# The 64-expert stage: second products in plain float32, subtractions on VectorE, outputs evicted on ScalarE, the gate at the end, empty slots not gathered

## The chip, the cores and the metric

One core of one Trainium2 chip runs the whole program. The metric is the device time of the core in microseconds (us). The time before is 3594.27 us, the median of 3 runs (3585.16 to 3597.85). Engines are named as in the profile: PE is TensorE, DVE is VectorE, ACT is ScalarE, POOL is GpSimd, SP is SyncE, which issues the weight loads.

## What is computed

The reference is two transformer blocks one after the other on 512 tokens of width 1024. Everything in the change lies in the last stage, the feed-forward part of the second block: 64 experts in 8 groups, 8 experts for each token, and one shared expert. Cut to that:

```python
def moe_ffn(h, router_w, router_bias, w_gu, w_dn, w_sh_gu, w_sh_dn):
    t = h.reshape(B * S, D)                                # 512 x 1024
    scores = jax.nn.sigmoid((t @ router_w).astype(jnp.float32))
    ...                                                    # top 4 of 8 groups, then top 8 experts
    top_w = top_w / jnp.sum(top_w, axis=-1, keepdims=True) * ROUTED_SCALE
    routed = routed_experts(t, top_i, top_w, w_gu, w_dn)   # 64 experts, hidden 256
    shared = swiglu(t, w_sh_gu, w_sh_dn).astype(jnp.float32)
    return (routed + shared).reshape(B, S, D).astype(h.dtype)

x = x + g2 * moe_ffn(...)          # g2 is the gate, one number for each of the 1024 columns
return rmsnorm_2(x, final_g)
```

512 tokens times 8 experts are 4096 pairs, so an expert has 64 tokens on average.

## The kernel before, in words

The stage is the class `Moe64`; its `run` is called last, after a stage that mixes tokens. The residual `xT` and the normed input `hT` lie transposed in SBUF (features on partitions).

Prologue: `start` turns the residual to token rows and writes it to a DRAM tensor `sum` of 512 + 128 rows (the last 128 are spare rows; their first content does not matter). `tokens` writes the normed input as rows to the DRAM tensor `rows`. `route` does the routing, a long run of small VectorE instructions. `shared_up` does the first product of the shared expert.

Then a loop over 65 blocks of 128 slots: one for each of the 64 experts, and one (`EXTRA`) that takes a second block of an expert with more than 128 tokens. The weights of an expert are three units of 1 MB (two of the first product, one of the second), each a [128, 2048] float32 tile. They come on SP's queue into a ring of slots (L240); a slot is loaded again when its last reader is done. In block e the program does, in this order:

- `up(e)`: 8 calls of `product`, one for each 128 rows of the contraction. `product` splits the weight piece (128x512 float32) in two float32r halves that together keep its precision: a copy on ScalarE rounds it (L532), and a subtraction makes the rest (L533), every third time on GpSimd, else on VectorE. Then come three matmuls (L2401, L2402, L2403). The two halves have four buffers each (`PIECES`). Silu on ScalarE (L2411) and a multiplication on VectorE (L2412) follow.
- `spread` of the output of block e - 2 (L2438): GpSimd issues a DMA that adds 128 rows of 4 KB to the rows of `sum` at the places `dst`. Each of these waits on GpSimd's queue until the one before it has landed, since both write `sum`. Empty slots (64 of 128 on average) add zeros to the spare rows.
- `down(e - 1)`: for each half of the columns two `product` calls, so 4 in all, and one VectorE instruction that multiplies by the slot's weight and by the gate row (L2433) into `y`, which has 3 buffers.
- `turn(e + 1)`: 8 transposes of the gathered rows and their split into two halves from PSUM (ScalarE and VectorE, 128x512, twice).
- `fetch(e + 4)`: a one-hot compare on VectorE (L2362), 4 small matmuls, six small VectorE instructions that make the slots' row numbers, and an indirect DMA on GpSimd's queue (L2378) that gathers 128 rows of 4 KB from `rows`; empty slots gather row 0. `AHEAD` is 4.
- `turn_hid(e)`: two transposes and their split (128x256).
- in blocks 4, 8, 12 and 16 also `shared_down`: 4 float32 matmuls (L2353) and 2 VectorE evictions with the gate into `sh`.

At the end, SP loads `sum` back (L2518), and for each of four row tiles VectorE adds `sh` (L2520), ScalarE squares and sums (L2521), VectorE scales (L2523) and SP stores the output.

The order within an engine is set ahead of time by priorities from this program order, so an instruction can move forward past others of its engine, but each engine then runs its list in order. An earlier stage, `HierMoe` (32 experts), gathers rows with the bounds check that the change brings here: an index beyond the last row moves nothing (L1357).

## Time and profile before

| | us |
|---|---|
| median of 3 runs | 3594.27 |
| the profiled execution | 3588.4 |
| its span in the trace | 3586.7 |
| stretch of the 65 blocks, first scatter-add to last (L2438) | 2763.0 to 3560.6 |
| PE, DVE, ACT, POOL busy over the span | 3167.3, 2079.6, 1510.7, 940.1 |

The page shows the span in 40 slices of 89.7 us; the stage of the change fills slices 31 to 40. Matmuls overlap each other in the records, so their spacing tells more than their length. A record of a DMA queue counts the time of its packets as a share of 16 DMA engines.

### The profile page before, as it was taken

How to read it: one execution, taken by the hardware profiler on the slowest of the kernel's cores; microseconds unless marked ns; L12 is line 12 of the kernel's file. 1: busy time of each engine (PE TensorE's matmuls, PEld its weight loads, DVE VectorE, ACT ScalarE, POOL GpSimd, SP SyncE). 2: the span in 40 equal slices, each digit the busy share in tenths (PEclk: the TensorE clock that was granted, in tenths of full speed). 3: DMA queues.
4: the chain of work that ended last, by engine and by line, in shares of the span. 5: the costliest groups of instructions: out<-in, count | busy, mean ns of one | idle time of the engine just before them, and what ended most of it. 6: DMA issues, size and time to landing. Idle time of an engine off the chain costs nothing. (4 is left out here: it accounts for less than half of the span.)

```text
span 3586.7 us, 46891 instructions
## 1 busy us (share of the span) xinstructions
PE 3167.3 (88%) x17204; PEld 1966.6 (55%) x17204; DVE 2079.6 (58%) x4291; ACT 1510.7 (42%) x2849; POOL 940.1 (26%) x932
## 2 busy tenths in 40 slices
PE   7888989979998998999899995899998888888885
PEld 4666767643333336763333332676565666666663
DVE  3677673543334335343333334564647999999996
ACT  5555554521111113331111111554545667777775
POOL 3544332100000000000000001221003666666664
PEclk9988999979999998989999997899999999999998
DMA  4111233468999993558999993114236999999996
GB/s 168 54 54 39 68 119 119 183 268 350 413 386 394 371 378 144 188 192 356 397 401 374 367 374 149 72 59 153 95 125 211 331 330 331 337 339 340 334 337 173
DMA packets 140714, 885.09 MB, mean 247 GB/s; under 512 B 19136, under 2 KB 19904, under 8 KB 46784
## 3 DMA queue, kind: packets, MB, share of 16 engines
q1 hardware_dynamic: 103824, 748.73, 53.5%
q0 software_dynamic: 34208, 124.28, 12.0%
q10 hardware_dynamic: 2448, 9.04, 0.7%
q8 instruction: 137, 2.24, 0.3%
q14 instruction: 97, 0.79, 0.1%
HBM read 836.10 MB, written 55.57 MB: 249 GB/s over the span
## 5 line engine op out<-in xcount | busy, mean ns | idle before, releaser
L532 ACT ACTIVATE phase<-arena 128x512 fp32r<-128x512 f32 (+1 forms) x989 | 608.9, 622 | 450.0 <-PE ps L545 196.6
L533 DVE TENSOR_TENSOR phase<-arena,phase 128x512 fp32r<-128x512 f32 (+1 forms) x663 | 612.0, 939 | 128.4 <-ACT phase L532 122.4
L533 POOL TENSOR_TENSOR phase<-arena,phase 128x512 fp32r<-128x512 f32 (+1 forms) x454 | 514.2, 1134 | 589.2 <-ACT phase L532 492.2
L545 PE MATMUL ps<-phase 128*128 128x512 f32 (+3 forms) x1000 | 394.6, 395 | 1.0 <-POOL phase L533 1.0
L1412 PE MATMUL ps<-arena 128*64 128x512 f32 x1008 | 346.3, 614 | 45.2 <-DVE arena L1402 45.2
L2403 PE MATMUL ps<-phase 128*128 128x512 f32 x780 | 312.7, 401 | 64.0 <-DVE phase L533 64.0
L2402 PE MATMUL ps<-phase 128*128 128x512 f32 x780 | 321.3, 412 | 45.1 <-DVE phase L533 33.9
L2401 PE MATMUL ps<-phase 128*128 128x512 f32 x780 | 312.7, 401 | 6.9 <-ACT phase L532 1.5
L1390 PE MATMUL ps<-arena,phase 128*64 128x512 f32 x968 | 303.6, 624 | 2.2 <-ACT phase L1369 0.7
L1390 PE MATMUL ps<-arena 128*64 128x512 f32 x1008 | 303.2, 617 | 1.9 <-DVE arena L1435 0.2
L544 PE MATMUL ps<-phase 128*128 128x512 f32 (+1 forms) x736 | 283.1, 385 | 24.0 <-DVE arena L1710 14.7
L1357 POOL DMA_INDIRECT phase<-hrows,phase x35 | 34.9, 997 | 951.0 <-DVE arena L1393 664.3
L546 PE MATMUL ps<-phase 128*128 128x512 f32 (+1 forms) x736 | 279.5, 380 | 1.1 <-POOL phase L533 1.1
L1392 ACT ACTIVATE arena<-ps 64x512 f32<-64x512 f32 x34 | 20.0, 589 | 477.1 <-PE ps L1390 477.1
L2402 PEld LDWEIGHTS ps<-phase 128*128 128x128 f32 x780 | 146.5, 188 | 128.8 <-DVE phase L533 64.6
L545 PEld LDWEIGHTS ps<-phase 128*128 128x128 f32 (+2 forms) x1000 | 192.4, 193 | 37.6 <-issue 3.3
L2403 PEld LDWEIGHTS ps<-phase 128*128 128x128 f32 x780 | 146.8, 188 | 113.6 <-DVE phase L533 89.5
L1435 DVE SCALAR_TENSOR_TENSOR arena<-ps,arena 128x512 f32<-128x512 f32 x280 | 190.7, 744 | 16.7 <-PE ps L1434 15.5
L1412 PEld LDWEIGHTS ps<-arena 128*64 128x64 f32 x1008 | 93.4, 138 | 179.6 <-issue 130.4
L1354 DVE COPY phase<-ps 128x2 f32<-128x2 f32 (+1 forms) x35 | 5.6, 159 | 304.7 <-PE ps L1352 303.6
L2401 PEld LDWEIGHTS ps<-phase 128*128 128x128 f32 x780 | 146.8, 188 | 48.5 <-ACT phase L532 18.5
L1390 PEld LDWEIGHTS ps<-arena 128*64 128x64 f32 x1008 | 87.6, 142 | 154.5 <-issue 148.6
(625 smaller groups left out, 5818.1 us busy)
## 6 DMA issues: line engine op xcount, KB each, us to landing
arena<-in_moe SPq DMA_DIRECT2D x550, 1024.0 KB, 8.8
arena<-in_ada SPq DMA_DIRECT2D x72, 1024.0 KB, 6.5
phase<-in_moe SPq DMA_DIRECT2D x26, 1024.0 KB, 11.3
arena<-in_wina SPq DMA_DIRECT2D x16, 1024.0 KB, 4.8
arena<-in_win SPq DMA_DIRECT2D x13, 1024.0 KB, 5.1
arena<-in_winb SPq DMA_DIRECT2D x12, 1024.0 KB, 5.8
arena<-in_wouta SPq DMA_DIRECT2D x4, 1024.0 KB
arena<-in_woutb SPq DMA_DIRECT2D x4, 1024.0 KB, 5.6
```

Source lines behind the costliest of these rows:

```text
L532: self.nc.scalar.activation(h, x, AF.Copy)
L533: (eng or self.nc.vector).tensor_tensor(l, x, h, op=OP.subtract)
L544: mm(ps, w[0], x[0], start=start, stop=False)
L545: mm(ps, w[0], x[1], start=False, stop=False)
L546: mm(ps, w[1], x[0], start=False, stop=stop)
L1357: nc.gpsimd.indirect_dma_start(out=x, out_offset=None, in_=self.rows[:], in_offset=bass.IndirectOffsetOnAxis(ap=idx[:n, :1], axis=0), boun ...
L1390: nc.tensor.matmul(ph[64 * j:64 * j + 64, :], x[:, k, :], u, start=k == 0, stop=k == 7)
L1412: nc.tensor.matmul(py[64 * j:64 * j + 64, :], hT[:, k, :], u, start=k == 0, stop=k == 3)
L1435: nc.vector.scalar_tensor_tensor(xT[:, f, :], ps, gate[:, f:f + 1], xT[:, f, :], op0=OP.mult, op1=OP.add)
L2401: nc.tensor.matmul(ps, x[0], h, start=start, stop=False)
L2402: nc.tensor.matmul(ps, x[0], l, start=False, stop=False)
L2403: nc.tensor.matmul(ps, x[1], h, start=False, stop=stop)
```

## The change

- `down` multiplies the hidden values as plain float32 with the weights as they were loaded: one float32 matmul (128x128 by 128x512) in place of a split and three float32r matmuls, 4 in place of 12 per block. `turn_hid` then only copies the transposed hidden values (ScalarE) and has no subtraction.
- `product` makes the rest (the subtraction) always on VectorE.
- The result of `down` is evicted by ScalarE with the slot's weight as its scale (2 instructions of 128x512); the gate is not applied there.
- `sum` starts with zeros (5 DMAs of a zeroed tile); the residual's rows go to another DRAM tensor `xrow`, from where one DMA on ScalarE's queue loads them into `sh`. `shared_down` adds the gated shared output to it (one more VectorE instruction per half). At the end VectorE multiplies the loaded sum by the gate, 4 instructions of 128x1024.
- `fetch` gives empty slots a row number beyond the last, with the bounds check, so that they are not gathered; the four tiles that receive the rows are zeroed once by GpSimd. The scatter-add still sends 128 rows.

```diff
--- before.py
+++ after.py
@@ -2168,7 +2168,6 @@
 EXTRA = 1
 SHARED = 4, 8, 12, 16
 PIECES = 4
-SHARE = 1, 3
 FAR = 1048576.0
 
 
@@ -2178,7 +2177,6 @@
 
     def __init__(self, K):
         self.K, self.nc, self.tc = K, K.nc, K.tc
-        self.turns = 0
 
     def route(self, hT):
         K, nc, a = self.K, self.nc, self.K.a
@@ -2317,6 +2315,9 @@
 
         K, nc = self.K, self.nc
         self.sum = K.dp.tile([T + P, D], F32, name="sum", bufs=1)
+        self.xrow = K.dp.tile([P, 4, D], F32, name="xrow", bufs=1)
+        for i in range(5):
+            nc.gpsimd.dma_start(self.sum[P * i:P * i + P], self.xr[0])
         for i in range(4):
             t = K.a.rot("tok", [P, D], 2)
             for half in range(2):
@@ -2324,8 +2325,7 @@
                 for k in range(4):
                     nc.tensor.transpose(p[:, P * k:P * k + P], xT[:, 4 * half + k, P * i:P * i + P], K.ident)
                 nc.scalar.activation(t[:, 512 * half:512 * half + 512], p, AF.Copy)
-            nc.gpsimd.dma_start(self.sum[P * i:P * i + P], t)
-        nc.gpsimd.dma_start(self.sum[T:], t)
+            nc.gpsimd.dma_start(self.xrow[:, i, :], t)
 
     def shared_up(self, hT):
 
@@ -2352,7 +2352,9 @@
             for k in range(2):
                 nc.tensor.matmul(p, self.hid[:, k, P * i:P * i + P], self.dn[:, 1024 * k + 512 * half:1024 * k + 512 * half + 512],
                                  start=k == 0, stop=k == 1)
-            nc.vector.tensor_tensor(self.sh[:, i, c], p, self.gate[:, c], op=OP.mult)
+            t = K.t2k()
+            nc.vector.tensor_tensor(t, p, self.gate[:, c], op=OP.mult)
+            nc.vector.tensor_tensor(self.sh[:, i, c], self.sh[:, i, c], t, op=OP.add)
 
     def fetch(self, pos, info):
 
@@ -2369,14 +2371,16 @@
         idx, dst = a.rot("idx", [P, 2], AHEAD + 2).bitcast(I32)[:, 0:1], a.rot("dst", [P, 2], AHEAD + 2).bitcast(I32)[:, 0:1]
         w = a.rot("w", [P, 1], AHEAD + 2)
         V.tensor_tensor(s[:, 6:7], s[:, 0:1], s[:, 1:2], op=OP.add)
-        V.tensor_copy(idx, s[:, 6:7])
         V.tensor_reduce(out=w, in_=s[:, 2:5], op=OP.add, axis=AX.X)
 
         V.tensor_scalar(s[:, 7:8], s[:, 5:6], -1.0, 1.0, op0=OP.mult, op1=OP.add)
+        V.scalar_tensor_tensor(idx, s[:, 7:8], 4096.0, s[:, 6:7], op0=OP.mult, op1=OP.add)
         V.scalar_tensor_tensor(dst, s[:, 7:8], self.spare, s[:, 6:7], op0=OP.mult, op1=OP.add)
-        x = a.rot("xr", [P, D], AHEAD)
+        self.row += 1
+        x = self.xr[self.row % AHEAD]
         nc.gpsimd.indirect_dma_start(out=x, out_offset=None, in_=self.rows[:],
-                                     in_offset=bass.IndirectOffsetOnAxis(ap=idx[:, :1], axis=0))
+                                     in_offset=bass.IndirectOffsetOnAxis(ap=idx[:, :1], axis=0),
+                                     bounds_check=T - 1, oob_is_err=False)
         return x, w, dst
 
     def turn(self, x):
@@ -2396,8 +2400,7 @@
 
         K, nc = self.K, self.nc
         h, l = (K.r.rot(n, [P, 512], PIECES) for n in ("wh", "wl"))
-        self.turns += 1
-        K.parts(h, l, w, nc.gpsimd if self.turns % SHARE[1] < SHARE[0] else nc.vector)
+        K.parts(h, l, w)
         nc.tensor.matmul(ps, x[0], h, start=start, stop=False)
         nc.tensor.matmul(ps, x[0], l, start=False, stop=False)
         nc.tensor.matmul(ps, x[1], h, start=False, stop=stop)
@@ -2417,9 +2420,9 @@
         pt = K.ps()[:, :256]
         for k in range(2):
             nc.tensor.transpose(pt[:, P * k:P * k + P], hid[:, P * k:P * k + P], K.ident)
-        parts = [K.r.rot(n, [P, 256], 1) for n in ("hh", "hl")]
-        K.parts(*parts, pt)
-        return parts
+        t = K.a.rot("hidT", [P, 256], 2)
+        nc.scalar.activation(t, pt, AF.Copy)
+        return t
 
     def down(self, hid, w, unit):
         K, nc, a = self.K, self.nc, self.K.a
@@ -2427,10 +2430,9 @@
         for half in range(2):
             py = K.ps()
             for k in range(2):
-                self.product(py, [t[:, P * k:P * k + P] for t in hid],
-                             unit[:, 1024 * k + 512 * half:1024 * k + 512 * half + 512], k == 0, k == 1)
-            c = slice(512 * half, 512 * half + 512)
-            nc.vector.scalar_tensor_tensor(y[:, c], py, w, self.gate[:, c], op0=OP.mult, op1=OP.mult)
+                nc.tensor.matmul(py, hid[:, P * k:P * k + P],
+                                 unit[:, 1024 * k + 512 * half:1024 * k + 512 * half + 512], start=k == 0, stop=k == 1)
+            nc.scalar.activation(y[:, 512 * half:512 * half + 512], py, AF.Copy, scale=w)
         return y
 
     def spread(self, y, dst):
@@ -2449,6 +2451,9 @@
         K.lane = ""
         K.normed(hT, xT, T, gain, shift)
         a.rot("tok", [P, D], 2)
+        self.xr, self.row = [a([P, D]) for _ in range(AHEAD)], 0
+        for t in self.xr:
+            nc.gpsimd.memset(t, 0.0)
         K.lane = "b"
         with K.tc.high_priority(-1000):
             self.start(xT)
@@ -2471,6 +2476,7 @@
         a.unrot("tok")
         self.sh, self.dn = a([P, 4, D]), a([P, ROW])
         nc.scalar.dma_start(self.dn, K.I["shdn"][0])
+        nc.scalar.dma_start(self.sh, self.xrow)
 
         def finish():
             hT, e, unit = last_e
@@ -2510,13 +2516,15 @@
         self.overflow()
         K.ring.give(spare)
         a.free(self.hid, self.dn)
-        a.unrot("oh", "slot", "idx", "dst", "w", "xr", "hid", "y")
-        K.r.unrot("xh", "xl", "wh", "wl", "hh", "hl")
+        a.unrot("oh", "slot", "idx", "dst", "w", "hid", "hidT", "y")
+        a.free(*self.xr)
+        K.r.unrot("xh", "xl", "wh", "wl")
         a.free(self.pos, self.info)
         s, q, r = a([P, 4, D]), a([P, D]), a([P, 4])
         for i in range(4):
             nc.sync.dma_start(s[:, i, :], self.sum[P * i:P * i + P])
         for i in range(4):
+            nc.vector.tensor_tensor(s[:, i, :], s[:, i, :], self.gate, op=OP.mult)
             nc.vector.tensor_tensor(s[:, i, :], s[:, i, :], self.sh[:, i, :], op=OP.add)
             nc.scalar.activation(q, s[:, i, :], AF.Square, accum_out=r[:, i:i + 1])
             K.rstd(r[:, i:i + 1], r[:, i:i + 1], 1.0 / D, K.eps)
```

## Rows read from the trace of the kernel before

**Rows 1.** The page: busy tenths of VectorE in 40 slices of the span
```profile
DVE  3677673543334335343333334564647999999996
```

**Rows 2.** Busy time by stretch: PE, PEld, DVE, ACT, POOL, clock, DMA share, GB/s
```profile
3000.00:3500.00 500.00, 423.74 (x2007) 310.21 (x2008) 493.60 (x843) 363.78 (x643) 329.58 (x241) 1.00 1.00 337
```

**Rows 3.** Groups, 3000 to 3500 us: count, busy, mean ns, idle before, releasers
```profile
L533 DVE TENSOR_TENSOR phase<-arena,phase 128x512 fp32r<-128x512 f32 x323 | 333.1, 1050 | 6.4 <-ACT phase L532 2.7
L532 ACT ACTIVATE phase<-arena 128x512 fp32r<-128x512 f32 x483 | 303.5, 632 | 135.6 <-issue 73.4 <-PE ps L2403 46.9
L533 POOL TENSOR_TENSOR phase<-arena,phase 128x512 fp32r<-128x512 f32 x161 | 208.4, 1295 | 133.3 <-ACT phase L532 132.5
...
L2433 DVE SCALAR_TENSOR_TENSOR arena<-ps,arena,phase 128x512 f32<-128x512 f32 x80 | 59.6, 745 | 0.0
L533 DVE TENSOR_TENSOR phase<-ps,phase 128x512 fp32r<-128x512 f32 x80 | 51.0, 676 | 0.0
```

**Rows 4.** Waits, 3000 to 3500 us: total, times, longest
```profile
PE ps L2403 <- DVE phase L533: 46.3, 40, 1.2
```

**Rows 5.** Timeline of one block: start, length, engine, instruction, idle before
```profile
3202.78 1.29 POOL L533 TENSOR_TENSOR phase<-arena,phase 128x512 fp32r<-128x512 f32 x1 [0.76 <-ACT phase L532]
...
3203.16 1.46 DVE L533 TENSOR_TENSOR phase<-arena,phase 128x512 fp32r<-128x512 f32 x1
...
3206.53 0.69 DVE L533 TENSOR_TENSOR phase<-arena,phase 128x512 fp32r<-128x512 f32 x1
```

**Rows 6.** Timeline of PE: two split matmuls, and seven float32 ones in a row
```profile
2738.92 0.39 PE L2402 MATMUL ps<-phase 128*128 128x512 f32 x1
2739.14 0.39 PE L2403 MATMUL ps<-phase 128*128 128x512 f32 x1
...
2697.07 3.18 PE L2340 MATMUL ps<-arena 128*128 128x512 f32 x7
```

**Rows 7.** All scatter-adds (L2438): lengths in ns, first and last start; time to landing
```profile
L2438 POOL DMA_INDIRECT sum<-arena x65: 1547/1847/1874, 2763.0 to 3560.6; - x65
...
DMA to landing us min/median/max: 6.3/10.8/12.6
```

**Rows 8.** The scatter-adds of 3017.5 and 3030.0 us, and the wait of the second
```profile
L2438 POOL DMA_INDIRECT sum<-arena x2: 1855/1856/1857, 3017.5 to 3030.0; - x2
L2438 POOLq EVENT_SEMAPHORE  x1: 17/17/17, 3029.2 to 3029.2; - x1
...
DMA to landing us min/median/max: 10.8/11.2/11.7
```

**Rows 9.** DMA queues, 3000 to 3500 us: packets, MB, share; issues to landing
```profile
q1 hardware_dynamic: 17280, 125.85, 66.6%
q0 software_dynamic: 11554, 42.08, 33.5%
...
sum<-arena POOLq DMA_INDIRECT x40, 11.0
```

**Rows 10.** DMA queues, 900 to 1000 us, in the stage with 32 experts
```profile
q1 hardware_dynamic: 5579, 40.61, 98.4%
q0 software_dynamic: 432, 0.72, 2.0%
...
phase<-hrows,phase POOLq DMA_INDIRECT x3, 8.7
```

**Rows 11.** Timeline: first gather of the stage, last scatter-add, additions at the end
```profile
2730.85 1.02 POOL L2378 DMA_INDIRECT arena<-rows,arena  x1 [21.99 <-DVE arena L2371]
...
3560.57 1.55 POOL L2438 DMA_INDIRECT sum<-arena  x1 [5.48 <-POOLq L2589]
...
3572.24 3.79 DVE L2520 TENSOR_TENSOR arena<-arena 128x1024 f32<-128x1024 f32 x3 [15.28 <-DMA arena<-sum]
```

**Rows 12.** Busy time by stretch around a fall of TensorE's clock, columns as in Rows 2
```profile
2743.90:2747.35 3.45, 1.35 (x15) 1.15 (x14) 3.45 (x5) 1.83 (x4) 1.72 (x2) 1.00 0.90 316
2747.35:2750.76 3.41, 3.41 (x12) 2.93 (x12) 2.18 (x11) 1.50 (x3) 0.95 (x1) 0.50 0.80 281
```

## The prediction

> **What bounds the kernel now.** I read the page's slices first, to find the stage. The reader is to see that VectorE is at 0.9 or more in eight slices at the end and nowhere else [rows 1]. Then the busy times of a stretch in the middle of the 65 blocks: in 500 us VectorE works 493.6 us, TensorE 423.7, ScalarE 363.8, GpSimd 329.6, and the DMA engines have a share of 1.00 [rows 2]. In these 500 us 40 scatter-adds are issued [rows 9], so a block takes 12.5 us and costs VectorE 12.3, TensorE 10.6, ScalarE 9.1 and GpSimd 8.2 us. Two resources are full, and a full one need not be the one that ends last. So I looked at the waits: TensorE waits for VectorE's subtractions once in each block, 46.3 us in 40 times [rows 4]. VectorE is what ends last now.
>
> Two things stand close behind it. First the DMA engines: weights take 0.666 of the stretch and GpSimd's gathers and scatter-adds 0.335 [rows 9], 8.33 and 4.19 us of a block. Second a chain that no busy share shows. Each scatter-add waits on GpSimd's queue for the landing of the one before. One issued at 3017.5 us landed 11.7 us later, at 3029.2; at that moment the wait of the next one ended, and it was issued at 3030.0 [rows 8]. So a block can't be shorter than a landing plus 0.8 us. Landings take 11.0 us in the middle of this stretch, 6.3 to 12.6 over all [rows 7, 9]: 11.8 us of the 12.5 that a block takes.
>
> **The change part by part, in one block of the stretch.**
>
> *Splits.* Before, VectorE makes 8 of 12 rests from SBUF and GpSimd 4. They disturb each other: a subtraction of VectorE beside one of GpSimd took 1.46 us, one without took 0.69 [rows 5], and the mean is 1.05 [rows 3]. After, 8 are left (those of `up`), all on VectorE, none on GpSimd, so each should take 0.69. VectorE: 333.1 / 40 = 8.33 becomes 8 x 0.69 = 5.52, a gain of 2.8. GpSimd loses 208.4 / 40 = 5.2 and keeps its two DMA issues, 3.0 us. ScalarE loses 4 x 0.63 = 2.5 [rows 3].
>
> *Evictions and hidden values.* L2433 leaves VectorE, 59.6 / 40 = 1.5 us. ScalarE gets two evictions of the same size; the trace has none of its own, I take the 0.63 us of its 128x512 copy [rows 3], so +1.3. The subtraction of `turn_hid` goes; it is half the size of one of 0.68 us from PSUM [rows 3], so some 0.4. One small index instruction replaces another. VectorE comes to 12.3 - 2.8 - 1.5 - 0.4 = 7.6 us, ScalarE to 9.1 - 2.5 + 1.3 = 7.9.
>
> *Products.* 12 split matmuls that follow each other after 0.22 us, 2.6 us, become 4 float32 ones; seven of that kind in a row took 3.18 us, so 0.45 each and 1.8 in all [rows 6]. TensorE comes to 10.6 - 0.8 = 9.8 us. The Trainium skill, page "FP8 and Floating Point Precision", section TensorE Precision Notes, says that true float32 takes four passes through the array. At four times the 0.22 us of a pass these products would take 3.5 us and TensorE 11.5; the trace does not agree, it shows two passes' time.
>
> *New waits.* ScalarE's evictions wait for the product and for a free `y` buffer, that is for the landing of the scatter-add three blocks back; behind them on ScalarE stand the copies of the next weight pieces, for which TensorE waits. With three buffers that landing is due two blocks earlier, so I cost it at nothing; without that cover it makes the block follow the scatter-adds, which it does anyway in my sum.
>
> *Gathers.* Half the slots are empty. In the earlier stage with the bounds check three gathers moved 0.72 MB in 2.0 us of all engines [rows 10], 59 rows of 4 KB each where 128 would be 0.52 MB; so a skipped row moves nothing, and a MB costs 2.8 us. Half a gather, 0.26 MB, saves 0.73 us of DMA time. The scatter-add stays at 128 rows.
>
> *What is late next.* The compute engines need about 10 us (TensorE 9.8; between that and 11.7, if TensorE loses 1.9 us to waiting as now). The DMA engines need 8.33 + 4.19 - 0.73 = 11.8 us at today's pace; at best weights go at the pace of the earlier stage, 98.4 us for 40.61 MB [rows 10], so 3.15 MB take 7.6 and the sum is 11.1. The scatter-adds need a landing plus 0.8 us: 11.8 if landings stay, since weights still stream beside them. I take 11.8 us for a block, from 11.1 (DMA at best) to 13.4 (every landing as long as the longest, 12.6).
>
> *Head and end.* Four more fills and four more DMA issues on GpSimd, 2 MB more written and 2 MB more read, all before the first gather. GpSimd was idle for 22.0 us before that gather, waiting for VectorE's routing [rows 11], which hides them; the load into `sh` waits on ScalarE's queue, with the next copies behind it, for `xrow` and for the place of `hT`. I take 2 us, from 0 to 7. At the end VectorE gets four instructions of 128x1024; three additions of that size took 3.79 us without a gap [rows 11], so 4 x 1.26 = +5 us, in the open. The eight additions in `shared_down` lie under VectorE's free time of 4 us in a block; without it they would cost 5.5 us in all.
>
> *Sum.* From the first scatter-add to the last there are 64 intervals, 797.6 us [rows 7]. At both ends of the stretch few weights stream and landings are short (6.3 at the least; the last scatter-add came 7.3 us after the one before, after an idle wait of 5.5 [rows 11]), so compute sets the pace there; I take 10 such intervals at 10.0 us, and 54 at 11.8: 737 us, a gain of 60. The two blocks ahead of the first scatter-add gain 2 x 2.5 = 5. Against it 5 at the end and 2 at the head. So 58 us: from 3588.4, the profiled execution's own time (1.7 us over its span), to 3530. The median of the runs lies 5.9 us above that execution; I go half of it and say 3533.
>
> **The rivals.**
> - *DMA sets the pace at its best.* With half the gather gone, landings shorten below 10.3 us and blocks take 11.1: 54 x 11.1 + 10 x 10 = 699, 98 us of gain in the stretch, net 96, about 3495, or 3485 if the light blocks take 9. For it: landings of 6.3 us where little streams. Against it: the 1.00 share, which says that the engines have no room to spare at today's pace. Chance 0.23.
> - *Slower: landings grow.* Weight slots come free earlier, so loads are queued more densely, and the scatter-adds wait behind them. With 12.6 us each the block takes 13.4: 54 x 13.4 + 100 = 824, 26 us more than now; with the head at 7 and the end at 5, less 5, 3624. It decides from a landing of 11.7 us on. For it: the spread of landings. Against it: loads are already never out. Chance 0.09.
> - *TensorE becomes the bound.* It would pause in each block, and the clock fell to half (0.50, 1.2 GHz) for 3.4 us after a stretch in which it was busy 1.35 of 3.45 us [rows 12], where it was 1.00 in the middle of the stage [rows 2]. One such fall costs 1.7 us of work: 9.8 + 1.7 = 11.5, still under 11.8; with the 0.8 us that one more wait may cost it is 12.3, and so is no gain but at the ends: 54 x 12.3 + 110 = 774, net 21, 3570. By the skill's four passes one fall would make 13.2 and the change a loss. Chance 0.18, half of it within the bound of no change.
>
> **How the numbers follow.** Forecast 0.50; rivals 0.23, 0.09 and 0.18. A measurement of this kernel tells about 0.3%, 11 us, from no change. Faster by more: 0.50 + 0.23 + 0.09 = 0.82; within: 0.09; slower: 0.09. The range takes in the forecast, the DMA rival and most of the third: 3482 to 3582.
>
> **What would show it.** Right: scatter-adds issued every 11.8 us in the middle, each 0.8 us after the landing of the one before; landings still near 11 us; VectorE's subtractions near 0.69 us, its busy share under 0.75; GpSimd's share halved; gathers of half the bytes; the four gate instructions back to back at the end. Wrong: landings under 10 (a larger gain) or over 11.7 us (a loss), a clock under 0.95 in the stretch, or TensorE waiting for ScalarE's copies behind evictions.

## The result, and the profile after

The kernel after takes 3504.12 us, the median of 4 runs (3496.06 to 3511.01), the kernel before 3594.18 (4 runs, 3585.16 to 3597.85): a ratio of 0.9752, 95% interval 0.9723 to 0.9781. The prediction said 3533, from 3482 to 3582. The profiled execution took 3507.6 us, its span is 3505.9.

The page first, busy tenths of TensorE and VectorE in 40 slices, as in [rows 1].

```profile
PE   7888999989898998999999897699999899999996
DVE  3667763543333335343333334456463777776675
```

VectorE is no longer at 9 anywhere in the last ten slices; TensorE is. Two stretches of the loop say how much. The columns are those of [rows 2].

```profile
2946.00:3100.00 154.00, 153.14 (x658) 102.43 (x657) 117.26 (x257) 112.35 (x199) 38.10 (x29) 1.00 1.02 360
3150.00:3400.00 250.00, 245.39 (x1033) 160.42 (x1033) 177.50 (x408) 177.98 (x316) 68.50 (x45) 0.99 1.02 358
```

TensorE is busy for 153.1 of 154 us in the first stretch, VectorE for 117.3, ScalarE for 112.4. GpSimd works a quarter of the time, where it worked two thirds [rows 2]. The DMA share is 1.02 and the rate 360 GB/s, where it was 1.00 and 337 [rows 2].

Groups of instructions from 2950 to 3400 us, columns as in [rows 3]; 41 scatter-adds (L2440) say that these are 41 blocks.

```profile
L533 DVE TENSOR_TENSOR phase<-arena,phase 128x512 fp32r<-128x512 f32 x329 | 216.3, 690 | 9.8 <-ACT phase L532 9.7
...
L2433 PE MATMUL ps<-arena 128*128 128x512 f32 x330 | 159.9, 607 | 1.2
L2440 POOL DMA_INDIRECT sum<-arena x41 | 66.7, 1627 | 316.0 <-ACT phase L532 144.8 <-DVE arena L2378 99.7 <-DVE phase L533 47.4
L2435 ACT ACTIVATE arena<-ps,arena 128x512 f32<-128x512 f32 x82 | 56.5, 689 | 43.4 <-PE ps L2433 43.4
```

A subtraction on VectorE takes 690 ns, an eviction on ScalarE 689. Most telling is L2433: 330 matmul records in 41 blocks, 8 in each, where the program issues 4.

The scatter-adds, over all the loop, and the start of silu (L2414), one in each block, which I use as the blocks' clock.

```profile
L2440 POOL DMA_INDIRECT sum<-arena x65: 1549/1586/2081, 2772.8 to 3476.8; - x65
...
DMA to landing us min/median/max: 6.2/10.1/11.4
L2414 ACT ACTIVATE arena<-ps x14: 386/386/387, 2951.8 to 3092.5; 128x256 f32<-128x256 f32 x14
L2414 ACT ACTIVATE arena<-ps x22: 385/386/387, 3157.1 to 3390.9; 128x256 f32<-128x256 f32 x22
```

From the first scatter-add to the last there are 704.0 us, where there were 797.6 [rows 7]: 11.0 us for each of 64 intervals, 12.46 before. Landings are 10.1 us in the median, 10.8 before. By silu a block takes (3092.5 - 2951.8) / 13 = 10.82 us in the first stretch and 233.8 / 21 = 11.13 in the second.

What sets these two paces stands in the chain of work that ended last: its shares by line, for a stretch up to 3150 us and one from there to 3330 (a piece that begins in a stretch counts whole), and of its pieces some of the longest, with start and length.

```profile
by line: PE ps L2433 26.4%; DMA sum<-arena 25.5%; PE ps L2404 14.1%; PE ps L2406 12.4%; PE ps L2405 12.3%; PE ps L2394 6.1%; PE ps L2422 1.9%; issue 1.8%; PE ps L2368 0.6%; ACT phase L532 0.3%; POOLq L2381 0.1%; POOLq L2440 0.0%
by line: DMA sum<-arena 69.2%; PE ps L2433 9.9%; PE ps L2405 5.1%; PE ps L2404 4.7%; PE ps L2406 4.6%; issue 3.7%; PE ps L2394 2.4%; DVE phase L533 1.9%; ACT phase L532 0.7%; PE ps L2422 0.7%; POOLq L2381 0.3%; PE ps L2368 0.2%; POOLq L2440
2768.36 3.44 PE ps L2433 x8
...
3092.46 2.58 PE ps L2433 x6
3099.19 10.77 DMA sum<-arena
3110.72 10.09 DMA sum<-arena
3121.58 10.03 DMA sum<-arena
...
3325.84 3.08 PE ps L2433 x6
```

The reader is to see three parts. From the first block to 3099 us the chain runs through TensorE's matmuls, block after block; L2404 to L2406 are the matmuls of `up`, L2394 the transposes. From 3099.2 to 3242, and again for some blocks up to 3321, it is scatter-adds that follow each other: issued at 3110.72 and 3121.58, 10.86 us apart, 10.09 of it a landing and 0.77 the way to the next issue. At the end it is TensorE again. So neither VectorE nor the DMA engines set the pace in most of the loop, and the chain of scatter-adds only in a part of it.

Outside the loop: the first instruction of the stage (an iota on GpSimd) in the kernel before and after, and the new gate instructions (L2527) among the additions (L2528) at the end.

```profile
L2274 POOL IOTA phase<- x1: 243/243/243, 2679.1 to 2679.1; 128x128 f32 x1
L2272 POOL IOTA phase<- x1: 243/243/243, 2688.8 to 2688.8; 128x128 f32 x1
3487.19 1.23 DVE L2527 TENSOR_TENSOR arena<-arena,phase 128x1024 f32<-128x1024 f32 x1 [20.02 <-DMA arena<-sum]
3488.45 1.23 DVE L2528 TENSOR_TENSOR arena<-arena 128x1024 f32<-128x1024 f32 x1
3489.59 2.36 DVE L2527 TENSOR_TENSOR arena<-arena,phase 128x1024 f32<-128x1024 f32 x2
3491.86 1.22 DVE L2528 TENSOR_TENSOR arena<-arena 128x1024 f32<-128x1024 f32 x1
```

The stage began 9.7 us later than before, after a part of the program that the change does not touch. There the same matmuls of L1987 ran from 2414.0 to 2438.1 us before and from 2412.6 to 2447.6 after, with a granted clock from 2405 to 2445 us of 0.96 and 0.66, so these 9.7 us are not the change's. From the iota to the first scatter-add it took 2763.0 - 2679.1 = 83.9 us before and 2772.8 - 2688.8 = 84.0 after. From the last scatter-add to the end it took 26.1 us before and 29.1 after, so the stage itself gained 90.5 us. The whole: -93.6 + 0.1 + 3.0 + 9.7 = -80.8 us, which is the difference of the two spans.

### The profile page after: what moved, and what is told of

Same layout as the page of the kernel before. It is cut to its first block, busy times and chain, and to the rows that moved or that the text cites. A ratio compares the mean times of both kernels' runs of the same rounds, so it can differ in the third digit from the quotient of the medians.

```text
span 3505.9 us, 45353 instructions
## 1 busy us (share of the span) xinstructions
PE 3192.4 (91%) x16944; PEld 1941.3 (55%) x16944; DVE 1823.6 (52%) x4108; ACT 1438.5 (41%) x2719; POOL 596.0 (17%) x680
## 3 DMA queue, kind: packets, MB, share of 16 engines
q0 software_dynamic: 34784, 109.10, 11.2%
q10 hardware_dynamic: 2592, 11.14, 0.9%
## 5 line engine op out<-in xcount | busy, mean ns | idle before, releaser
L532 ACT ACTIVATE phase<-arena 128x512 fp32r<-128x512 f32 (+1 forms) x729 | 448.1, 618 | 355.4 <-PE ps L545 196.3
L533 DVE TENSOR_TENSOR phase<-arena,phase 128x512 fp32r<-128x512 f32 (+1 forms) x663 | 436.6, 681 | 124.1 <-ACT phase L532 122.9
L2433 PE MATMUL ps<-arena 128*128 128x512 f32 x520 | 250.4, 605 | 2.5 <-ACT arena L2424 0.8
L533 POOL TENSOR_TENSOR phase<-arena,phase 128x256 fp32r<-128x256 f32 (+1 forms) x194 | 173.6, 896 | 373.1 <-ACT phase L532 247.9
L2406 PE MATMUL ps<-phase 128*128 128x512 f32 x520 | 228.0, 438 | 0.0
L2404 PE MATMUL ps<-phase 128*128 128x512 f32 x520 | 212.0, 408 | 2.4 <-ACT phase L532 0.5
L2405 PE MATMUL ps<-phase 128*128 128x512 f32 x520 | 205.4, 395 | 6.5 <-DVE phase L533 6.4
L2440 POOL DMA_INDIRECT sum<-arena x65 | 105.3, 1619 | 494.3 <-ACT phase L532 168.6
L544 PEld LDWEIGHTS ps<-phase 128*128 128x128 f32 x736 | 139.3, 189 | 56.4 <-ACT phase L532 20.3
L1390 PEld LDWEIGHTS ps<-arena,phase 128*64 128x64 f32 x968 | 86.6, 142 | 148.2 <-issue 142.5
## 6 DMA issues: line engine op xcount, KB each, us to landing
phase<-in_moe SPq DMA_DIRECT2D x26, 1024.0 KB, 11.2
```

The source lines that it names most:

```text
L532: self.nc.scalar.activation(h, x, AF.Copy)
L533: (eng or self.nc.vector).tensor_tensor(l, x, h, op=OP.subtract)
L544: mm(ps, w[0], x[0], start=start, stop=False)
L1390: nc.tensor.matmul(ph[64 * j:64 * j + 64, :], x[:, k, :], u, start=k == 0, stop=k == 7)
L2404: nc.tensor.matmul(ps, x[0], h, start=start, stop=False)
L2405: nc.tensor.matmul(ps, x[0], l, start=False, stop=False)
```

## The experiments

Twelve kernels ran: ten from the kernel after with something undone, taken away or added, two from the kernel before. "Block" is the time from silu to silu, worked out as above, in the two stretches. The ratio is to runs of the kernel before that were made alongside (medians from 3585.3 to 3600.0 us), so rows are better compared by ratio than by us.

| | us | ratio to before, 95% | block 2946 to 3100 | block 3150 to 3400 |
|---|---|---|---|---|
| before | 3594.2 | 1 | 12.56 | 12.49 |
| after | 3504.1 | 0.9752 (0.9723 to 0.9781) | 10.82 | 11.13 |
| gather of all rows | 3510.1 | 0.9766 (0.9749 to 0.9782) | 10.90 | 11.22 |
| scatter-add of filled slots only | 3495.5 | 0.9727 (0.9702 to 0.9752) | 10.82 | 10.75 |
| two sums | 3515.3 | 0.9772 (0.9731 to 0.9812) | 10.82 | 10.92 |
| before with two sums | 3600.5 | 1.0000 (0.9980 to 1.0021) | 12.57 | 12.45 |
| no scatter-adds | 3493.7 | 0.9718 (0.9672 to 0.9764) | 10.82 | 10.75 |
| a third of the rests on GpSimd | 3528.2 | 0.9806 (0.9765 to 0.9847) | 11.31 | 11.34 |
| second products split again | 3523.8 | 0.9808 (0.9763 to 0.9853) | 11.14 | 11.70 |
| half of the second products | 3507.0 | 0.9770 (0.9736 to 0.9803) | 10.97 | 11.76 |
| half of them, two sums | 3508.6 | 0.9776 (0.9743 to 0.9808) | 11.33 | 11.15 |
| eviction on VectorE | 3504.6 | 0.9777 (0.9739 to 0.9815) | 10.87 | 11.21 |
| half split, filled slots only | 3500.7 | 0.9749 (0.9733 to 0.9765) | 10.42 | 11.27 |
| before, all rests on VectorE | 3588.4 | 0.9989 (0.9971 to 1.0006) | 12.61 | 12.61 |

My theories after the result: the chain of scatter-adds sets the block (theory 1), the DMA engines do (theory 2), TensorE does (theory 3).

### Gathers of all rows, and scatter-adds of filled slots only

The first undoes the skipped gathers. The second keeps them skipped and lets the scatter-add skip the empty slots too.

```diff
-        V.scalar_tensor_tensor(idx, s[:, 7:8], 4096.0, s[:, 6:7], op0=OP.mult, op1=OP.add)
+        V.tensor_copy(idx, s[:, 6:7])
...
-                                     in_offset=bass.IndirectOffsetOnAxis(ap=idx[:, :1], axis=0),
-                                     bounds_check=T - 1, oob_is_err=False)
+                                     in_offset=bass.IndirectOffsetOnAxis(ap=idx[:, :1], axis=0))
```

> The changed kernel with one part undone: empty slots gather row 0 again, 128 rows per gather. Theory 1 (the chain of scatter-adds sets the pace: each waits for the landing of the one before, landing plus 0.76 us): landings go from 10.3 back to 11.0 us, blocks from 11.1 to 11.8, 54 dense intervals cost 38 us more, about 3543. Theory 2 (the DMA engines' throughput sets the pace): the 0.26 MB more per gather cost 0.73 us a block, 40 us, about 3545; the distance from a landing to the next issue would then vary. Theory 3 (TensorE, whose busy share is 0.99, sets the pace): 3504, no change.

```diff
-        V.scalar_tensor_tensor(dst, s[:, 7:8], self.spare, s[:, 6:7], op0=OP.mult, op1=OP.add)
+        V.scalar_tensor_tensor(dst, s[:, 7:8], 4096.0, s[:, 6:7], op0=OP.mult, op1=OP.add)
...
-                                          in_=y, in_offset=None, compute_op=OP.add)
+                                          in_=y, in_offset=None, compute_op=OP.add,
+                                          bounds_check=T - 1, oob_is_err=False)
```

> The changed kernel, and the scatter-add skips empty slots too (about 64 of 128 rows move). Theory 1: 64 packets fewer of 0.33 us on 16 engines, landings 1.3 us shorter, the chain needs 9.8 us, and the block falls to 10.0 (compute) at the least: 50 to 65 us less, 3440 to 3455. Theory 2 (DMA throughput): the engines need 1.3 us less, about 9.9, the same time, but the distance from landing to issue would vary. Theory 3 (TensorE): 3504.

By theories 1 and 2 the first should have been at some 3543 and the second at 3440 to 3455; 3510 and 3495 were measured. Theory 3, 3504 for both, is 6 us off the one and 9 off the other. Stretches of the first, then of the second kernel, and the shares of the second one's last-ending chain:

```profile
3150.00:3400.00 250.00, 244.71 (x1024) 157.48 (x1025) 168.68 (x403) 175.87 (x312) 68.91 (x44) 1.00 1.03 374
3150.00:3400.00 250.00, 248.60 (x1069) 166.24 (x1068) 189.35 (x422) 183.61 (x325) 66.69 (x48) 1.00 0.98 346
by line: PE ps L2433 34.8%; PE ps L2404 19.4%; PE ps L2405 16.9%; PE ps L2406 16.9%; PE ps L2394 8.2%; PE ps L2422 2.6%; PE ps L2368 0.7%; issue 0.6%
```

Two things follow. With all rows gathered, the DMA engines move 374 GB/s at a share of 1.03, and the block takes only 0.1 us more. The kernel before has the same transfers in a block, at 337 GB/s and a share of 1.00 [rows 2]; a share of 1.00 was no limit there. And with fewer rows to add, the chain that ended last holds matmuls alone, every block takes 10.75 to 10.82 us in both stretches, and the time falls by 9 us in the medians (the intervals overlap), not by 50: something that has nothing to do with rows stops it at 10.75. The chain (from 2950 to 3400 us) shows matmuls there, and theory 3 gains.

### Two sums, after and before

The scatter-adds go to two tensors in turn, so each waits for the one two blocks back. Both are zeroed ahead of the loop, and loaded and added at the end, which costs time there (the last scatter-add to the end: 36.9 us, 29.1 after).

```diff
-        self.sum = K.dp.tile([T + P, D], F32, name="sum", bufs=1)
+        self.sums = [K.dp.tile([T + P, D], F32, name="sum" + n, bufs=1) for n in "ab"]
...
-        self.nc.gpsimd.indirect_dma_start(out=self.sum[:], ...
+        self.sent += 1
+        self.nc.gpsimd.indirect_dma_start(out=self.sums[self.sent % 2][:], ...
```

> The changed kernel with two sum tensors that the scatter-adds use in turn, so that each waits for the landing of the one two blocks back; at the end both are loaded and added (4 more loads and 4 more additions, about +7 us). Theory 1 (the chain, a landing of 10.3 us plus 0.77, sets the block): the chain is cut, blocks fall to what TensorE needs, about 10.3 to 10.5 us (its records follow each other in 10.2 us of the 11.05), so some 54 x 0.6 to 0.75 = 32 to 40 us less and 7 more: 3470 to 3485. Theory 2 (the DMA engines are full and the landing is only what is left over): the block stays at 11.0 us, landings grow past 11 us without anyone waiting for them, time 3504 + 7 = 3511. Theory 3 (TensorE, 99% busy by its records, sets the block): the same 3511, with blocks of 11.0 us.

> The kernel before with two sum tensors that the scatter-adds use in turn, both loaded and added at the end (about +7 us). If VectorE sets the block of the kernel before (12.3 of 12.5 us busy), blocks stay at 12.4 to 12.5 us and the time is 3594 + 7 = 3601. If the chain of scatter-adds (11.05 us landing plus 0.8, 11.8, with up to 1.5 us from landing to issue) sets it, blocks fall to 12.3 or less and the time is 3594 - 10 + 7 = 3591 or less.

With the chain cut in the kernel after, blocks take 10.82 us in the first stretch, no less than with it, and 10.92 in the second, where they had taken 11.13. The time, 3515, is what theories 2 and 3 expected. Theory 1 falls as the one cause: the chain costs some 0.2 us a block late in the loop. In the kernel before, blocks stay as they were, 12.57 and 12.45 us, and VectorE stays full. (The whole time doesn't decide there: at 1.0000 it lies between the two expectations, and its interval is 7 us to either side.)

```profile
3150.00:3400.00 250.00, 211.99 (x1008) 154.97 (x1004) 248.02 (x422) 182.67 (x323) 166.86 (x121) 1.00 1.01 338
```

So the chain did not set the pace of the kernel before. Nor did the DMA engines, which move the same transfers at 374 GB/s in the run that gathers all rows. VectorE, busy for 248 of 250 us, is what is left, as the prediction's first part says.

### No scatter-adds

Only the first of the 65 scatter-adds is sent; the others are left out, so most of the routed sum is missing from the output.

```diff
+        self.sent = getattr(self, "sent", 0) + 1
+        if self.sent > 1:
+            return
         self.nc.gpsimd.indirect_dma_start(out=self.sum[:], ...
```

> The changed kernel with only the first scatter-add; the other 64 are left out, so most of the routed sum is missing from the output. 128 rows of 4 KB per block, about 2.6 us of the DMA engines, and the whole chain are gone. Theories 1 and 2: the block falls to what the compute engines need, TensorE about 10.3 us, and the time to 3504 - 64 x 0.75 = 3455 (3440 to 3465). Theory 3 (TensorE needs the full 11.0 us): 3495 to 3505. A TensorE that needs 9.8 us, as the prediction had it, would give 3504 - 64 x 1.2 = 3427.

```profile
3150.00:3400.00 250.00, 248.54 (x1067) 165.84 (x1067) 190.47 (x423) 183.31 (x326) 22.82 (x24) 1.00 0.85 318
L2414 ACT ACTIVATE arena<-ps x23: 386/386/387, 3156.7 to 3393.3; 128x256 f32<-128x256 f32 x23
```

Without the chain and with a DMA share of 0.85, a block takes 236.6 / 22 = 10.75 us, and TensorE is busy for 248.5 of 250 us. That is TensorE's own need, not the 10.2 to 10.3 that I had read from the spacing of its records: the time is 3494, not 3455.

### Half of the second products, alone and with two sums

To see what stands behind TensorE, its work is cut: of the second products only the first half of the contraction is made (the other half of the sum is left out of the output), 2 float32 matmuls in a block in place of 4.

```diff
-            for k in range(2):
+            for k in range(1):
...
-                                 unit[...], start=k == 0, stop=k == 1)
+                                 unit[...], start=True, stop=True)
```

> The changed kernel with only the first half of the contraction in the second products (2 of 4 float32 matmuls per block; the other half of the sum is left out of the output). TensorE's own need falls by 2 x 0.86 = 1.72 to 9.0 us, nothing else changes. If TensorE alone sets the block (10.75 us), blocks fall to 9.0 to 9.3 us and the time to 3395 to 3420. If the chain of scatter-adds stands close behind (landing 10.3 plus 0.77 = 11.05 us), the blocks run ahead at first, until the few buffers of row numbers are used up, and then go at 10.8 to 11.1 us: 3480 to 3504. If the DMA engines are full (share 1.02), the same 3480 to 3504, with landings of over 11 us.

> The same (half of the contraction left out) with two sum tensors used in turn, which cost 11 us in the run with two sums alone. If the chain set the pace of the run with half the contraction, blocks now fall toward 9.0 to 10 us and the time is 20 to 80 us under that run. If the DMA engines did, blocks stay where they were and the time is 5 to 15 us above that run.

The shares of the last-ending chain from 2950 to 3400 us, and waits from 3150 to 3400 us (engine, place, releaser: us in total, times, longest), first with one sum, then with two:

```profile
by line: DMA sum<-arena 89.7%; issue 5.4%; DVE phase L533 1.5%; PE ps L2405 1.5%; PE ps L2406 1.3%; ACT phase L532 1.1%; PE ps L2404 1.1%; POOLq L2381 0.5%; PE ps L2394 0.3%; ACT arena L2435 0.3%; PE ps L2433 0.2%; DVE arena L2364 0.1%; POO
DVE arena L2378 <- DMA sum<-arena: 48.5, 21, 3.8
by line: DMA arena<-in_moe 76.2%; DVE phase L533 7.0%; PE ps L2435 5.4%; PE ps L2406 4.3%; PE ps L2408 3.7%; PE ps L2407 3.7%; ACT phase L532 3.4%; PE ps L2396 0.9%; issue 0.7%; DVE arena L2417 0.5%; DVE arena L2366 0.4%; PE ps L2424 0.4%; 
ACT phase L532 <- DMA arena<-in_moe: 33.0, 24, 2.8
SPq L240 <- DMA arena<-in_moe: 95.5, 46, 3.5
```

TensorE's need fell by 2 x 0.86 us to some 9.0 us (an estimate), and nothing was gained: 3507 and 3509 us, against the 3395 to 3420 of theory 3 alone. With one sum the chain of scatter-adds takes 89.7% of what ended last; VectorE waits at L2378, where it writes the row numbers `dst`, for a landing that frees their buffer, 48.5 us in 21 times. With two sums the weights' loads take 76.2%; ScalarE waits for them 24 times and SP's queue is held by loads that have not landed. Each of the two limits is 11 to 11.8 us a block, TensorE's granted clock having fallen now and then, too (0.97 in both from 3150 to 3400 us, 0.98 and 0.94 from 2946 to 3100). So three limits lie within some 5% of each other: TensorE 10.75, a landing plus 0.77 some 10.9 to 11.3 (landings of 10.1 after, 10.5 here), the weights' loads about 11.15 beside two sums. The last is not the most that the DMA engines can move: it goes with 359 GB/s, and the kernel that gathers all rows moved 374. What holds the loads at that pace is not shown.

That also explains how the kernel after can take 10.82 us in the first stretch, less than two of its three limits: the first 17 blocks with their shared-expert products are longer for TensorE (by silu 2761.3 to 2951.8, 11.2 us each), and in them the transfers get ahead. The lead is then used up. From the end of a block's second eviction to its scatter-add 0.3 to 0.9 us pass in blocks 16 to 19 and 3.4 in block 29, whose scatter-add of 3099.19 us is the one from which the chain of the kernel after is made of landings; in block 36 it is 4.7.

### Undoing the parts on the compute engines

Second products split again as before (`turn_hid` makes its two halves again, too), subtractions on VectorE:

```diff
-                nc.tensor.matmul(py, hid[:, P * k:P * k + P], unit[...], start=k == 0, stop=k == 1)
+                self.product(py, [t[:, P * k:P * k + P] for t in hid], unit[...], k == 0, k == 1)
```

> The changed kernel with its second products split again, 12 float32r matmuls in place of 4 float32 ones and the subtractions on VectorE. TensorE's own need falls from 10.75 to about 9.9 us a block, VectorE's rises from 8.05 to about 8.05 + 4 x 0.69 + 0.4 = 11.2 us. If the slowest engine sets the block (TensorE now, VectorE then), blocks go to 11.2 to 11.4 us and the time to 3515 to 3535. If only the chain of scatter-adds counts, blocks stay at 11.05 us and the time at 3504.

Every third subtraction on GpSimd again:

```diff
-        K.parts(h, l, w)
+        self.turns += 1
+        K.parts(h, l, w, nc.gpsimd if self.turns % SHARE[1] < SHARE[0] else nc.vector)
```

> The changed kernel with every third of its 8 subtractions per block back on GpSimd. VectorE's own sum is still far below the block (about 5 x 0.69 to 1.4 plus 2 us), so VectorE cannot set it. If work on GpSimd delays the issue after a landing (1.49 us on average before, 0.77 after) and makes landings longer (11.05 before, 10.3 after), the block becomes 11.8 to 12.4 us and the time 3504 + 54 x 0.8 to 1.3 = 3547 to 3575. If landings were shorter for another reason (weights loaded earlier or fewer bytes), landings stay at 10.3 and the time is 3504 to 3530.

The output evicted on VectorE again:

```diff
-            nc.scalar.activation(y[:, 512 * half:512 * half + 512], py, AF.Copy, scale=w)
+            nc.vector.tensor_scalar(y[:, 512 * half:512 * half + 512], py, w, None, op0=OP.mult)
```

> The changed kernel with the outputs evicted on VectorE in place of ScalarE (2 instructions of 128x512 per block, about 1.5 us): VectorE 9.55 us a block, ScalarE 6.7, both under TensorE's 10.75. If TensorE and the chain set the pace, the time stays at 3504 within 10 us, and this move is worth nothing by itself. If VectorE's order matters (subtractions late behind evictions), blocks grow by up to 0.75 us: up to 3550.

Rows of each: the first kernel's late stretch, the second's two kinds of subtraction from 2946 to 3100 us, the third's first stretch and the shares of its last-ending chain.

```profile
3150.00:3400.00 250.00, 221.14 (x1071) 169.54 (x1070) 221.53 (x491) 211.24 (x387) 99.19 (x43) 0.99 0.99 339
L533 DVE TENSOR_TENSOR phase<-arena,phase 128x512 fp32r<-128x512 f32 x72 | 66.2, 947 | 24.1 <-ACT phase L532 23.8
L533 POOL TENSOR_TENSOR phase<-arena,phase 128x512 fp32r<-128x512 f32 x36 | 45.6, 1271 | 22.1 <-ACT phase L532 21.9
2946.00:3100.00 154.00, 151.89 (x653) 100.97 (x652) 131.22 (x286) 94.87 (x170) 41.15 (x28) 1.00 1.02 359
by line: DMA sum<-arena 87.7%; issue 5.5%; PE ps L2433 2.2%; PE ps L2404 1.0%; PE ps L2405 1.0%; PE ps L2406 1.0%; PE ps L2394 0.6%; POOLq L2381 0.6%; DVE phase L533 0.5%; POOLq L2440 0.1%; PE ps L2422 0.1%; PE ps L2368 0.1%; DVE arena L237
```

Split again, the time is 3524, inside what was expected for the slowest engine, but not by its mechanism alone: the blocks are longer late in the loop than VectorE's work, which leaves it idle for 28 of 250 us there, and landings are 46.5% of its last-ending chain from 2950 to 3400 us, VectorE's subtractions 10.2%. Every third subtraction on GpSimd costs some 20 us (0.9806 against 0.9752): VectorE's own take 947 ns on average in place of 690, GpSimd's 1271, TensorE waits for both (5.5 us in 9 times for GpSimd's in the first stretch), and landings (10.2 us there) are no longer. The intervals of both kernels overlap a little with that of the kernel after; the blocks of the first stretch, 11.14 and 11.31 us against 10.82, show the loss more clearly. That was within the second expectation, 3504 to 3530. The eviction's place is worth nothing measurable: VectorE has room for it, 131.2 of 154 us. In that kernel landings hold 87.7% of the last-ending chain at the same total time, which again shows how near the limits lie.

### TensorE's need lowered, with everything still computed

Filled slots only in the scatter-add, and of the two column halves of the second product one split, one in plain float32:

```diff
+                if half:
+                    self.product(py, [t[:, P * k:P * k + P] for t in hid[1]], w512, k == 0, k == 1)
+                else:
+                    nc.tensor.matmul(py, hid[0][:, P * k:P * k + P], w512, start=k == 0, stop=k == 1)
```

> The changed kernel with empty slots skipped by the scatter-add too, and of the two column halves of the second product one in plain float32 and one split: TensorE's own need falls from 10.75 to about 10.75 - 0.43 = 10.3 us a block, VectorE's rises to about 9.8, ScalarE's to 9.7. If TensorE alone set the 10.77 us of every block in the run with the skipped scatter-add, blocks go to 10.3 to 10.4 us and the time from 3495 to 3470 or 3475. If the DMA engines (a share of 0.98 to 1.0 there, so 10.6 us) or the chain (landing 9.98 plus 0.77, 10.75) are the floor, the time stays at 3485 to 3497.

```profile
L2414 ACT ACTIVATE arena<-ps x14: 385/385/387, 2956.4 to 3091.9; 128x256 f32<-128x256 f32 x14
by line: DMA sum<-arena 66.9%; PE ps L2404 7.1%; PE ps L2405 6.8%; PE ps L2406 6.5%; PE ps L2439 5.8%; issue 3.5%; PE ps L2394 2.6%; DVE phase L533 0.9%; PE ps L2422 0.8%; ACT phase L532 0.8%; POOLq L2381 0.3%; PE ps L2368 0.2%; POOLq L2445
```

In the first stretch a block takes 135.5 / 13 = 10.42 us, as expected of a TensorE that needs 0.4 us less. From 3110 us on landings take its place for most of the time and the block takes 11.27. The shares above are those from 3090 to 3330 us. The total, 3501, is above both expectations, 5 us above the kernel with filled slots only and level with the kernel after (0.9749 and 0.9752). So the lowest median of all complete kernels is that with filled slots only, 3495.5; its interval (0.9702 to 0.9752) overlaps that of the kernel after, so I don't call it faster.

### Before, with all subtractions on VectorE

One part of the change alone: in the kernel before, GpSimd makes no subtractions.

```diff
-        K.parts(h, l, w, nc.gpsimd if self.turns % SHARE[1] < SHARE[0] else nc.vector)
+        K.parts(h, l, w)
```

> The kernel before with one part of the change alone: all 12 subtractions of a block on VectorE, none on GpSimd. If the two disturb each other as the prediction has it (1.05 us on average beside GpSimd, 0.69 without), 12 x 0.69 = 8.3 us is what 8 x 1.05 = 8.4 was, VectorE stays at 12.3 us a block and the time at 3580 to 3600, with GpSimd free. If they don't disturb each other (a subtraction stays at 1.05 us), VectorE needs 16.5 us a block and the time is 3800 or more. If GpSimd's subtractions made the landings long (11.05 us before, 10.3 after), landings here are 10.3 us; if the load of the transfers did, they stay near 11 us.

```profile
L533 DVE TENSOR_TENSOR phase<-arena,phase 128x512 fp32r<-128x512 f32 x432 | 280.4, 687 | 19.4 <-ACT phase L532 19.3
3150.00:3400.00 250.00, 216.44 (x982) 167.06 (x982) 235.53 (x497) 175.93 (x316) 59.31 (x40) 0.93 1.00 332
DMA to landing us min/median/max: 6.6/8.0/10.1
```

12 subtractions at 687 ns take as long as 8 at 1050 [rows 3] did, and the time is the same (0.9989, interval 0.9971 to 1.0006). GpSimd's help was worth nothing, since it slowed VectorE by as much as it took off it. (One thing differs beside it: the granted clock is 0.93 here and was 1.00, and VectorE is busy for 235.5 of 250 us. What that cost this kernel is not separated.) What I had not foreseen: landings are 8.0 us here, 11.0 in the kernel before in the same stretch, at the same DMA share of 1.00 and nearly the same rate. So in this kernel taking the subtractions off GpSimd made landings 3 us shorter. By what way is not shown, and it does not carry over: with GpSimd as free, landings are 10.1 us in the kernel after, at 358 to 360 GB/s, and 9.9 in the kernel with the products split again, at 339 GB/s and blocks of 11.7 us (below, 3150 to 3400 us).

```profile
DMA to landing us min/median/max: 9.7/9.9/11.4
```

No part by itself carries the gain of 90 us. Undone in the kernel after, each gives back 0 to 24 us in the medians, since other limits stand close by. This kernel and the one with the products split again both make 12 subtractions on VectorE and lie 0.018 apart in the ratio, 65 us; between them lie above all the evictions, 1.5 us of VectorE in a block [rows 3], and the gathers. That the evictions bring most of it is an inference: no run took them alone out of the kernel before.

## Why the prediction was right, and where it was not

The direction, the range and the first part (VectorE ends last before) hold. The size was off, 90 us in place of 58 to 61, and two steps under it failed in opposite directions. So the time lies in the range in part by luck: the limit of 11.8 us a block on which the forecast rests was not there, TensorE, which sets the pace for most of the loop, stood at 9.8 us in the sum, and the range holds the result because it also takes in the rival with faster transfers.

**VectorE and GpSimd: right.** A subtraction takes 0.69 us; VectorE falls to shares of 0.76 and 0.71 in the two stretches, where the prediction had it under 0.75, so the first just misses; GpSimd's share falls from 0.66 to 0.25 and 0.27, more than the half that was said. Two kernels show the contention from both sides: a subtraction takes 947 ns in the kernel after with a third of them on GpSimd, and 687 in the kernel before with none there. An eviction on ScalarE took 0.69 us, where 0.63 was taken. The Trainium skill, page "SBUF — State Buffer", section Who interferes with whom, says that a two-input VectorE instruction with both inputs in SBUF contends with GpSimd's reads; the 947 and 687 ns agree.

**Products: failed.** The prediction took 0.45 us for a float32 matmul from seven records in 3.18 us [rows 6] and had TensorE gain 0.8 us a block. A float32 matmul leaves two records. The trace of before shows it where the program can be counted: `shared_down` issues 4 matmuls for each of 4 row tiles, 16 in all, and its line has 32 records.

```profile
L2353 PE MATMUL ps<-phase,arena x32: 592/592/697, 2799.6 to 2956.6; 128*128 128x512 f32 x32
```

So it takes 3.44 us for 4 (the piece of the chain at 2768.36 us, 8 records), 0.86 each and not 0.45. TensorE lost 0.8 us on the products where the sum had it gain 0.8: it needs 10.75 us a block, not 9.8. The start of that sum was off as well, the other way: 10.6 us is the busy time of the records. Counted back from 10.75, with 3.44 us for the float32 products in place of 2.6, TensorE's need before was some 9.9 us (an estimate). The Trainium skill, page "FP8 and Floating Point Precision", section TensorE Precision Notes, has four passes for true float32; 0.86 is about four times the 0.22 of a pass [rows 6], so the trace agrees. The prediction weighed that rule and held the trace against it; the rule was right and the reading of the row wrong. Its sentence that TensorE would then take 11.5 us, and a fall of the clock make it 13.2, was too high, since it started from 10.6: 10.75 was measured, and in the kernel after the clock stayed at 1.00 in the first stretch and 0.99 in the second. The rival "TensorE becomes the bound" had the right engine for most of the loop, and a price (12.3 us a block) that it never came to.

**DMA engines and landings: failed, the other way.** The forecast held that the engines had no room at a share of 1.00, so 11.8 us, and that landings stay at 11.0, so again 11.8. The run that gathers all rows moved 374 GB/s at a share of 1.03 where the kernel before moved 337 at 1.00. Landings were 10.1. These 0.7 to 1 us in each of 54 blocks are where the larger gain comes from. The rival "DMA at its best" had it nearly right: landings below 10.3, blocks of 11.1 and 699 us for the loop, where 10.1, 11.0 and 704.0 were measured. But its reason is not the one that held: it had the DMA engines set the pace, and for most of the loop TensorE does. Why landings were shorter stays open. In the kernel before, taking the subtractions off GpSimd brought them from 11.0 to 8.0; in the kernel after, putting a third of them back left landings at 10.2 us in the first stretch, as they were. And a lower rate does not make them 8.0 either, as the 9.9 us at 339 GB/s of the split kernel show.

**The chain of scatter-adds: right in form.** Each is issued 0.77 us after the landing before it, as said, where the chain holds. But it holds in a part of the loop only, and cutting it gains some 0.2 us a block late in the loop, less than the second sum costs, since two other limits stand beside it.

**The new wait: another one.** The prediction looked at the `y` buffers on ScalarE. What holds the compute engines where the chain is made of landings is VectorE's write of `dst` (L2378), whose buffer is free when the scatter-add that reads it has landed; behind it stand the next subtractions, for which TensorE waits. From 3150 to 3400 us in the kernel after:

```profile
DVE arena L2378 <- DMA sum<-arena: 28.3, 21, 3.4
```

**Gathers: right in bytes, small in time.** 17.64 MB in 250 us on GpSimd's queue, 22.5 blocks, is 0.78 MB a block, 0.26 less than before. Undoing that costs 6 us by the medians, and the intervals overlap.

```profile
q0 software_dynamic: 6511, 17.64, 32.5%
```

**Head, light blocks and end.** From the stage's first instruction to its first gather it took 0.9 us longer than before, where the sum had 2; the two blocks from there to the first scatter-add gained 0.7 and not 5. Together that is the 0.1 measured. The end cost 3 us and not 5, as the gate instructions run between the additions and partly under the loads. The ten light intervals came out near their 100 us, but by two misses that cancel. The first five took 56.6 us (2772.8 to 2829.4), as TensorE sets the pace there too: 10.8 to 10.9 each, and 13.4 for the one with a shared-expert product. The last five took 45.7 (3431.1 to 3476.8), where little streams. The 54 between took 601.7 us, 11.14 each in place of 11.8, and hold the whole miss of the loop. The scatter-adds that end the first five and begin the last five:

```profile
2829.44 1.58 POOL L2440 DMA_INDIRECT sum<-arena  x1 [6.66 <-ACT arena L2435]
...
3431.12 1.58 POOL L2440 DMA_INDIRECT sum<-arena  x1 [8.40 <-ACT phase L532]
```

## What to carry to other kernels

A share of 1.00 is a limit only if the rate no longer rises when more is asked; compare GB/s under a heavier load before costing at the present pace. Count an instruction's records against what the program issues before a duration is taken from their number. Where several resources stand within a few per cent, taking away one shows nothing: read the chain that ended last stretch by stretch, and cut two at once to see the third.

## What the runs showed of the hardware

- A 128x128 by 128x512 float32 matmul takes 0.86 us at the full clock and leaves two records; a float32r one takes 0.22 [rows 6].
- The DMA share stood between 0.99 and 1.03 from 332 to 374 GB/s, so it told nothing of the room left in that band.
- In the kernel before, a scatter-add of 128 rows of 4 KB landed in 11.0 us (median) with a third of the subtractions on GpSimd and in 8.0 us with none, with the same transfers beside it and nearly the same rate (336 and 332 GB/s). In the kernel after, putting a third back changed little (10.2 and 10.2 us in the first stretch, 10.1 and 10.4 in the second), so it is no general price.
- With only the filled half of the rows sent, landings were still 10.1 us in the median (below, from the kernel with one half split, 2946 to 3100 us), against 10.2 with all rows in the kernel after: half the rows took nothing off a landing.

```profile
DMA to landing us min/median/max: 8.1/10.1/11.3
```
